# SwiGLU by seven products: eight pairs instead of seven, and ten chunks of the output product instead of nine

## The chip, the cores and the metric

The kernel runs on one core of a Trainium2 chip. The metric is the device time of one execution in microseconds (us), as the median of several runs. TensorE is called PE in the profile, its weight load PEld, VectorE DVE, ScalarE ACT, GpSimd POOL and SyncE SP.

## The reference

One layer of a streaming encoder for 256 rows of 2048 float32 values. What the change touches is the feed-forward part at its end; the mixer ahead of it gives x.

```python
h = rms_norm(x, norm_ffn[l])
gate_up = jnp.einsum('btd,df->btf', h, w_ffn_in[l])      # 2048 -> 2 x 5632
ff_gate, ff_up = jnp.split(gate_up, 2, axis=-1)
x = x + jnp.einsum('btf,fd->btd', jax.nn.silu(ff_gate) * ff_up, w_ffn_out[l])   # 5632 -> 2048
```

Ahead of it stand an RMS norm, one input projection (w_in), a gated recurrence and a chunked attention, their projections (w_pa, w_pb), gates, and an output projection (w_out) with a residual addition.

## The kernel before

**Products in float32.** TensorE multiplies in a reduced format. So every operand is cut in two halves, high and low: ScalarE writes the high half (a cast), VectorE subtracts it from the source for the low half (`load_weights` L151 and L152, `split` L183 and L184). One product of a 128x128 activation tile with a 128x512 weight tile is then a triple of matmuls, high x high, high x low, low x high (L174 to L176 in `product`, L229 to L231 in `product_pair`).

**Tiles.** Weights come by DMA from SP's queue in blocks of 512 KB (`fetch`, tile raw, 8 places): 128 partitions, two k-tiles, 512 columns. The halves have 7 places each (whi, wlo). A chunk is 512 rows of a weight, four k-tiles. The 256 rows of the activations are two row halves m. Activations lie transposed as high and low tiles (xT, x2T, hT), in the pool big, whose 25 places of 4 KB a partition also hold most other tiles.

**Seven products for eight.** `product_pair` does two column blocks at once. In a plain chunk this takes 16 triples. Where a chunk has a form (a tile with sums of its first two k-tiles' activations, made by `act_forms`), `seven` does the first two k-tiles by Strassen's scheme in Winograd's order: seven products of sums for the 2 x 2 x 2 blocks. Four of them (1, 5, 6, 7) are collected over all chunks in four PSUM banks of their own (ub, from the pool u_pool) and added behind the last chunk that has a form (`four_sums`, `residual_sums`); the others go straight to the result banks (cb, from c_pool). PSUM's eight banks are two pools of four, mm and aux. The weights' sums are made by `weight_forms` (L200) on VectorE.

**The stages.** In the feed-forward part, eleven steps j each make one 512-column block of the gate and one of the up part of w_fi over 4 chunks, by `swiglu_pair` where j is in SEVEN_IN and by two plain products otherwise. `here` and `other`, the two PSUM pools, change places at each j. The result hn is transposed by TensorE and split into hT[j] (`transpose_split`, L293, L302, L303). Where two seven pairs follow each other, this step of the first is put off (`late`, list `then`) until the sums of the second. For j in SEVEN the form of hT[j] is made too and written to DRAM (`kept`); for j in AWAY (0 to 3) hT[j] itself is written to DRAM (`put_away`) and loaded back later. Then two pairs of column blocks of w_fo run over the eleven chunks in the order 4 to 10, 0 to 3 (`ORDER`); each loads its forms one by one through `form_loader` (pool form, two places) on SP's queue. `again` loads hT[0..3] and the x for the residual addition on POOL's queue.

**The order of the work.** The instructions of an engine stand in an order that a planner chooses at compile time: by priority, which falls in the order of writing, from a simulation of the times. Weight preparation is written with a raised priority (PREP_AHEAD). Generators that were started move on by one step at each tick; a tick comes after every four triples. A tile that finds no free place in its pool makes its first writer wait. `keep_in_program_order` keeps a DMA on its queue in the written order.

Of the kernel before, what the change touches and what calls it, by code (L numbers as in the profile page):

```python
# [30 lines left out]
NPAR = 58  # L31

PREP_AHEAD = 500
N_WARM = 5

ORDER = (4, 5, 6, 7, 8, 9, 10, 0, 1, 2, 3)
SEVEN = ORDER[1:10]
AWAY = (0, 1, 2, 3)  # L40


SEVEN_IN = (1, 2, 4, 5, 7, 8, 10)
SEVEN_GATE = (1, 3)
SEVEN_OUT = (0,)

# [2 lines left out]
def block_kernel(ctx: ExitStack, tc: tile.TileContext, x, x_t, w_in, w_pa, w_pb, w_out, w_fi, w_fo,  # L49
# [3 lines left out]
    wraw_p = ctx.enter_context(tc.tile_pool(name="wraw", bufs=8))  # L53
    whi_p = ctx.enter_context(tc.tile_pool(name="whi", bufs=7))
    wlo_p = ctx.enter_context(tc.tile_pool(name="wlo", bufs=7))
    big = ctx.enter_context(tc.tile_pool(name="big", bufs=25))
    form_p = ctx.enter_context(tc.tile_pool(name="form", bufs=2))
    small = ctx.enter_context(tc.tile_pool(name="small", bufs=4))
    t6_p = ctx.enter_context(tc.tile_pool(name="t6", bufs=2))
    t2_p = ctx.enter_context(tc.tile_pool(name="t2", bufs=3))  # L60
# [6 lines left out]
    def nm(s):  # L67
        uid[0] += 1
        return f"{s}_{uid[0]}"

    def t4(shape, s, dt=F32):
        return big.tile(shape, dt, tag="t4", name=nm(s))
# [24 lines left out]
    warm_ps = aux.tile([P, 512], F32, tag="bank", name="warm_ps")  # L97
    for _ in range(N_WARM):
        nc.tensor.matmul(warm_ps[:, 0:256], lhsT=warm[:, 0:P], rhs=warm, start=True,
# [22 lines left out]
    def start(g):  # L122
        running.append(g)
# [160 lines left out]
    def split_tiles(s):  # L284
        return (t4([P, 4, T], s + "h", F32R), t4([P, 4, T], s + "l", F32R))
# [29 lines left out]
    def transpose_split(nat, hi, lo, gain=None, wait=2, pool=aux, forms=None, spill=None):  # L315
        for _ in range(wait):
            yield 1
        for pair in range(2):
            pt = transpose_split_pair(nat, pair, hi, lo, gain, pool)
            if forms is not None and pair == 0:  # L320
                act_forms(pt, forms, gain)
                if spill is not None:
                    nc.gpsimd.dma_start(out=spill, in_=forms.bitcast(F32))
            yield 1
# [23 lines left out]
    def form_loader(src):  # L348

        def get():  # L350
            f = form_p.tile([P, 2, 4, P], F32R, tag="form", name=nm("sf"))
            nc.sync.dma_start(out=f.bitcast(F32), in_=src)
            return f
        return get
# [536 lines left out]
    def swiglu_pair(j, c_pool, u_pool, then):  # L891
        hn = t4([P, 2, 512], "hn")
        u = []

        def sums(ub):
            u.extend(t2([P, 512], "u") for _ in range(2))
            four_sums(ub, hn[:, 0, :], hn[:, 1, :], *u)

            for g in then:
                start(g)  # L900

        cb = product_pair(w_fi, (j, NJ + j), 4, act_x2, fx, c_pool, u_pool, sums,
                          plain_first=True, last=True)
        for m in range(2):
            add(hn[:, m, :], cb[m, 0], hn[:, m, :])
            nc.scalar.activation(hn[:, m, :], hn[:, m, :], AF.Silu, scale=r2[:, m:m + 1])
        for m in range(2):
            add(u[m], cb[m, 1], u[m])
            up_times(hn, m, u[m])
        return hn  # L910
# [13 lines left out]
    for j in range(NJ):  # L924
        here, other = pools[j % 2], pools[1 - j % 2]
        if j in SEVEN_IN:
            hn = swiglu_pair(j, here, other, then)
# [10 lines left out]
        f = spill = None  # L938
        if j in SEVEN:
            f = t4([P, 2, 4, P], "sform", F32R)  # L940
            spill = kept[j] = dram.tile([P, 2, 4, P], F32, tag=f"kept{j}", name=nm("kept"))
        seven_next = j + 1 in SEVEN_IN or j + 1 == NJ
        late = j in SEVEN_IN and j + 1 in SEVEN_IN
        g = transpose_split(hn, *hT[j], forms=f, spill=spill, wait=0 if seven_next else 2,
# [9 lines left out]

    def again(nbs, xs, js):

        for _ in range(6):
            yield 1
        for j in js:
            hT[j] = split_tiles("hT")  # L960
            for d, dst in zip(away[j], hT[j]):
                tc.keep_in_program_order(nc.gpsimd.dma_start(out=dst.bitcast(F32), in_=d))
        for nb in nbs:
            xs[nb] = t4([P, 2, 512], "x2")
            tc.keep_in_program_order(nc.gpsimd.dma_start(out=xs[nb], in_=x2_kept[nb]))

    for pair in range(2):
        nbs = (2 * pair, 2 * pair + 1)
        xs = {}
        start(again(nbs, xs, AWAY if pair == 0 else ()))  # L970
        forms = {j: form_loader(kept[j]) for j in SEVEN}
        cb = product_pair(w_fo, nbs, NJ, act_h, forms, pools[1 - pair], pools[pair],
                          residual_sums(xs, nbs), last=pair == 1, chunks=ORDER)
        for n, nb in enumerate(nbs):
            for m in range(2):
                pieces = 2 if nb == 3 and m == 1 else 1
                w = 512 // pieces
                for i in range(pieces):
                    sl = slice(i * w, (i + 1) * w)
                    add(xs[nb][:, m, sl], cb[m, n][:, sl], xs[nb][:, m, sl])  # L980
                    nc.sync.dma_start(out=out_v[:, m, nb * 512 + i * w:nb * 512 + (i + 1) * w],
                                      in_=xs[nb][:, m, sl])
# [63 lines left out]
```

## Time and profile before

| | us |
|---|---|
| median of 3 runs (1418.93 to 1419.85) | 1419.33 |
| the profiled execution | 1418.53 |
| its span, from the first to the last instruction | 1416.5 |
| PE busy in it | 1408.3 |
| VectorE busy | 1119.3 |
| ScalarE busy | 791.7 |

The profile is of one execution. The engines run side by side, so busy times are not added. A row of the timeline gives start, length, engine, line, operation and tiles, with the number of equal instructions merged (x3); in square brackets stands how long the engine was idle before it and what ended that. Matmuls overlap, and the pace is the distance of their starts.

### The profile page before, as it was taken

The numbers are of one execution on the slowest core, as the hardware profiler recorded it, in microseconds if no ns is written. First come the engines' busy times: TensorE is split into PE (matmuls) and PEld (weight loads), VectorE is DVE, ScalarE is ACT, GpSimd is POOL, SyncE is SP. The second block draws the span as 40 slices with busy tenths as digits, with TensorE's granted clock in tenths as the row PEclk, the third lists the DMA queues.
The fourth block names the chain that finished last, engine by engine and source line by source line (L and its number), as shares of the span: only waits on it lengthen the run. The fifth ranks groups of instructions, "written<-read, shape, count | busy, mean of one in ns | idle before, by whom it ended". The sixth has DMA issues, their size and how long they took to land.

```text
span 1416.5 us, 17818 instructions
## 1 busy us (share of the span) xinstructions
PE 1408.3 (99%) x6412; PEld 1170.3 (83%) x6412; DVE 1119.3 (79%) x1459; ACT 791.7 (56%) x1038; POOL 61.1 (4%) x82
## 2 busy tenths in 40 slices
PE   9999999999999999999999999999999999999998
PEld 7888888888888888888888888888888888788887
DVE  6868869555878687779767987998699789889885
ACT  7756655565556464446654655655456455554652
POOL 0100100101100001120000000000000000100000
PEclk9999999999999999999999999999999999999999
DMA  9754454455868566557655677656576646988771
GB/s 359 279 193 160 150 182 156 153 185 189 263 217 296 188 237 237 196 166 236 245 199 178 208 267 253 215 197 221 178 243 236 225 162 209 346 306 313 248 260 56
DMA packets 88327, 311.96 MB, mean 220 GB/s; under 512 B 9904, under 2 KB 10160, under 8 KB 88240
## 3 DMA queue, kind: packets, MB, share of 16 engines
q1 hardware_dynamic: 82016, 288.29, 59.0%
q0 software_dynamic: 6224, 22.55, 4.2%
q8 instruction: 50, 0.82, 0.2%
q14 instruction: 37, 0.30, 0.1%
HBM read 295.60 MB, written 15.20 MB: 219 GB/s over the span
## 4 chain that ended last, share of the span: by engine, by line
PE 98%; DMA 1%; SPq 0%; ACT 0%; issue 0%; DVE 0%; DVEq 0%
PE mm L174 16%; PE mm L176 16%; PE mm L175 16%; PE mp L229 15%; PE mp L230 15%; PE mp L231 15%; PE bank L293 2%; PE bank L559 1%; DMA sf<-kept 1%; DMA xt<-in_x_t 1%; PE bank L589 0%; PE bank L635 0%; PE bank L686 0%; PE bank L714 0%; PE bank L724 0%; PE bank L726 0%
## 5 line engine op out<-in xcount | busy, mean ns | idle before, releaser
L152 DVE TENSOR_TENSOR wlo<-raw,whi 128x1024 fp32r<-128x1024 f32 (+1 forms) x260 | 311.9, 1209 | 132.9 <-ACT whi L151 130.8
L151 ACT CAST whi<-raw 128x1024 fp32r<-128x1024 f32 (+1 forms) x260 | 267.3, 1038 | 232.8 <-PE mm L176 152.4
L183 ACT CAST whi<-raw 128x1024 fp32r<-128x1024 f32 x248 | 230.5, 951 | 175.4 <-PE mp L231 85.9
L184 DVE TENSOR_TENSOR wlo<-raw,whi 128x1024 fp32r<-128x1024 f32 x248 | 267.5, 1098 | 48.5 <-ACT whi L183 47.5
L174 PE MATMUL mm<-whi,xTh 128*128 128x512 f32 x576 | 227.8, 400 | 0.8 <-ACT whi L151 0.8
L176 PE MATMUL mm<-whi,xTl 128*128 128x512 f32 x576 | 225.5, 391 | 0.0
L175 PE MATMUL mm<-wlo,xTh 128*128 128x512 f32 x576 | 225.4, 391 | 0.0
L174 PEld LDWEIGHTS mm<-whi,xTh 128*128 128x128 f32 x576 | 108.6, 189 | 23.0 <-ACT whi L151 2.0
L176 PEld LDWEIGHTS mm<-whi,xTl 128*128 128x128 f32 x576 | 108.5, 188 | 22.7
L175 PEld LDWEIGHTS mm<-wlo,xTh 128*128 128x128 f32 x576 | 108.7, 189 | 21.8 <-DVE wlo L152 0.7
L230 PE MATMUL mp<-wlo,x2Th 128*128 128x512 f32 x308 | 120.4, 391 | 0.0
L231 PE MATMUL mp<-whi,x2Tl 128*128 128x512 f32 x308 | 119.8, 390 | 0.0
L229 PE MATMUL mp<-whi,x2Th 128*128 128x512 f32 x308 | 111.2, 392 | 0.0
L183 ACT CAST whi<-tb 128x1024 fp32r<-128x1024 f32 x58 | 60.9, 1050 | 80.1 <-DVE tb L200 43.5
L230 PE MATMUL mp<-wlo,hTh 128*128 128x512 f32 x262 | 101.9, 389 | 0.0
L231 PE MATMUL mp<-whi,hTl 128*128 128x512 f32 x262 | 101.9, 389 | 0.0
L174 PE MATMUL mm<-whi,x2Th 128*128 128x512 f32 x256 | 100.0, 391 | 0.0
L175 PE MATMUL mm<-wlo,x2Th 128*128 128x512 f32 x256 | 99.8, 390 | 0.0
L176 PE MATMUL mm<-whi,x2Tl 128*128 128x512 f32 x256 | 99.8, 390 | 0.0
L184 DVE TENSOR_TENSOR wlo<-ta,whi 128x1024 fp32r<-128x1024 f32 x58 | 70.8, 1220 | 35.8 <-ACT whi L183 35.7
L229 PE MATMUL mp<-whi,hTh 128*128 128x512 f32 x262 | 97.0, 389 | 0.0
L183 ACT CAST whi<-ta 128x1024 fp32r<-128x1024 f32 x58 | 60.9, 1050 | 51.0 <-PE mp L231 28.6
(257 smaller groups left out, 2406.4 us busy)
## 6 DMA issues: line engine op xcount, KB each, us to landing
raw<-in_w_fi SPq DMA_DIRECT2D x176, 512.0 KB, 4.9
raw<-in_w_in SPq DMA_DIRECT2D x172, 512.0 KB, 4.3
raw<-in_w_fo SPq DMA_DIRECT2D x88, 512.0 KB, 5.4
raw<-in_w_out SPq DMA_DIRECT2D x32, 512.0 KB, 4.8
sf<-kept SPq DMA_DIRECT2D x18, 512.0 KB, 6.0
raw<-in_w_pa SPq DMA_DIRECT2D x16, 512.0 KB, 4.5
raw<-in_w_pb SPq DMA_DIRECT2D x16, 512.0 KB, 4.5
kept<-sform POOLq DMA_DIRECT2D x9, 512.0 KB, 4.4
```

The source lines that it names most:

```text
L151: nc.scalar.copy(hi[:, sl, :], src[:, sl, :])
L152: nc.vector.tensor_tensor(out=lo[:, sl, :], in0=src[:, sl, :], in1=hi[:, sl, :].bitcast(F32), op=ALU.subtract)
L174: nc.tensor.matmul(ps[m], lhsT=ah, rhs=wh, start=kc == 0 and k4 == 0, stop=False)
L175: nc.tensor.matmul(ps[m], lhsT=ah, rhs=wl, start=False, stop=False)
L176: nc.tensor.matmul(ps[m], lhsT=al, rhs=wh, start=False, stop=kc == n_chunks - 1 and k4 == 3)
L183: nc.scalar.copy(hi, src)
L184: nc.vector.tensor_tensor(out=lo, in0=src, in1=hi.bitcast(F32), op=ALU.subtract)
L229: nc.tensor.matmul(ps, lhsT=ah, rhs=wh, start=first, stop=False)
L230: nc.tensor.matmul(ps, lhsT=ah, rhs=wl, start=False, stop=False)
L231: nc.tensor.matmul(ps, lhsT=al, rhs=wh, start=False, stop=final)
L293: nc.tensor.transpose(out=pt[:, j, m * P:(m + 1) * P], in_=nat[:, m, c:c + P], identity=ident)
L559: nc.tensor.matmul(pl[:, j, :], lhsT=ek[:, g // 2, (g % 2) * P:(g % 2 + 1) * P], rhs=eq[:, g, :], start=True, stop=True)
```

## The change

The list of seven pairs becomes 1, 2, 3, 5, 6, 7, 9, 10: eight instead of seven, with three in a row twice. The output product's chunk 3, the last of the order, also gets a form, so that ten of eleven chunks are done by seven products, and the sums of the collected banks move into that last chunk. The pool form gets a third place and big loses one. `again` waits five ticks ahead of each of the four hT blocks and of x, where it waited six ticks once and then loaded all. One more warm-up product (128x256, on zeros) stands at the start.

```diff
-N_WARM = 5
+N_WARM = 6
 ORDER = (4, 5, 6, 7, 8, 9, 10, 0, 1, 2, 3)
-SEVEN = ORDER[1:10]
+SEVEN = ORDER[1:]
 AWAY = (0, 1, 2, 3)
-SEVEN_IN = (1, 2, 4, 5, 7, 8, 10)
+SEVEN_IN = (1, 2, 3, 5, 6, 7, 9, 10)
@@
-    big = ctx.enter_context(tc.tile_pool(name="big", bufs=25))
-    form_p = ctx.enter_context(tc.tile_pool(name="form", bufs=2))
+    big = ctx.enter_context(tc.tile_pool(name="big", bufs=24))
+    form_p = ctx.enter_context(tc.tile_pool(name="form", bufs=3))
@@ def again(nbs, xs, js):
-        for _ in range(6):
-            yield 1
         for j in js:
+            for _ in range(5):
+                yield 1
             hT[j] = split_tiles("hT")
             for d, dst in zip(away[j], hT[j]):
                 tc.keep_in_program_order(nc.gpsimd.dma_start(out=dst.bitcast(F32), in_=d))
+        for _ in range(5):
+            yield 1
         for nb in nbs:
             xs[nb] = t4([P, 2, 512], "x2")
```

## Rows read from the trace of the kernel before

**Rows 1.** The page: busy us, share of the span, instructions of each engine.

```profile
PE 1408.3 (99%) x6412; PEld 1170.3 (83%) x6412; DVE 1119.3 (79%) x1459; ACT 791.7 (56%) x1038; POOL 61.1 (4%) x82
```

**Rows 2.** Waits of PE, whole run: us in total, times, longest.

```profile
PE mp L229 <- DMA sf<-kept: 2.4, 1, 2.4
PE warm_ps L99 <- DVE warm L96: 1.2, 1, 1.2
PE mm L174 <- ACT whi L151: 0.8, 2, 0.7
```

**Rows 3.** Timeline of PE in the last chunk: start us, length us, instruction.

```profile
1404.35 0.39 PE L229 MATMUL mp<-whi,hTh 128*128 128x512 f32 x1
...
1405.03 0.39 PE L229 MATMUL mp<-whi,hTh 128*128 128x512 f32 x1
```

**Rows 4.** Windows: length, then busy us by engine, PEclk, DMA share, GB/s.

```profile
798.00:839.50 41.50, 41.50 (x187) 34.30 (x187) 39.78 (x47) 25.13 (x28) 0.00 (x0) 1.00 0.61 205
839.50:862.00 22.50, 22.50 (x107) 18.76 (x105) 17.26 (x28) 12.47 (x17) 2.66 (x5) 1.00 0.78 273
...
1305.00:1395.00 90.00, 90.00 (x399) 74.55 (x398) 76.20 (x84) 51.89 (x54) 0.00 (x0) 1.00 0.65 222
```

**Rows 5.** The chain of waits, 1205 to 1230 us: start, length, what.

```profile
1214.65 8.41 DMA sf<-kept
```

**Rows 6.** Waits of SP's queue, 1183 to 1300 us: us in total, times, longest.

```profile
SPq L352 <- PE mp L231: 31.4, 8, 7.6
```

**Rows 7.** Timeline of POOL: first and last load of the burst, 11 in all.

```profile
1212.45 0.53 POOL L962 DMA_DIRECT2D hTh<-h  x1
...
1225.63 0.53 POOL L965 DMA_DIRECT2D x<-x  x1 [1.93 <-issue]
```

**Rows 8.** Windows, the stretch behind that burst (columns as in rows 4).

```profile
1222.00:1246.00 24.00, 22.89 (x101) 18.97 (x102) 17.82 (x20) 11.92 (x13) 1.06 (x2) 1.00 1.03 418
```

**Rows 9.** Tile hTh on PE: length ns min/median/max, first and last start us.

```profile
L229 PE MATMUL mp<-whi,hTh x262: 389/389/476, 1181.8 to 1411.8; 128*128 128x512 f32 x131
```

**Rows 10.** Timeline of DVE in steady w_fo.

```profile
1336.70 0.68 DVE L200 TENSOR_TENSOR ta<-raw 128x512 f32<-128x512 f32 x1
1337.30 1.22 DVE L184 TENSOR_TENSOR wlo<-raw,whi 128x1024 fp32r<-128x1024 f32 x1
1338.44 0.68 DVE L200 TENSOR_TENSOR tb<-ta,raw 128x512 f32<-128x512 f32 x1
```

**Rows 11.** Timelines of DVE and PE, early in pair j=2.

```profile
810.47 3.49 DVE L184 TENSOR_TENSOR wlo<-raw,whi 128x1024 fp32r<-128x1024 f32 x3
...
814.60 0.39 PE L230 MATMUL mp<-wlo,x2Th 128*128 128x512 f32 x1
```

**Rows 12.** Timeline of PE at the start.

```profile
1.18 4.63 PE L99 MATMUL warm_ps<-warm 128*128 128x256 f32 x10 [1.18 <-DVE warm L96]
...
6.49 1.22 PE L174 MATMUL mm<-whi,xTh 128*128 128x512 f32 x2 [0.67 <-ACT whi L151]
...
14.04 0.73 PE L174 MATMUL mm<-whi,xTh 128*128 128x512 f32 x2 [0.16 <-ACT whi L151]
```

**Rows 13.** Timeline of DVE at the end: the last addition.

```profile
1412.71 0.76 DVE L103 TENSOR_TENSOR x<-mp,x 128x256 f32<-128x256 f32 x2 [2.03 <-PE mp L231]
```

**Rows 14.** Timelines of DVE and PE, from pair j=2 to pair j=3.

```profile
837.17 0.68 DVE L103 TENSOR_TENSOR hn<-mp,u 128x512 f32<-128x512 f32 x1
...
839.70 0.48 PE L174 MATMUL mm<-whi,x2Th 128*128 128x512 f32 x1
...
840.49 0.40 PE L174 MATMUL mm<-whi,x2Th 128*128 128x512 f32 x1
840.70 0.68 DVE L103 TENSOR_TENSOR u<-mp,u 128x512 f32<-128x512 f32 x1
...
842.43 0.68 DVE L303 TENSOR_TENSOR hTl<-bank,hTh 128x512 fp32r<-128x512 f32 x1
...
846.74 0.28 DVE L333 TENSOR_TENSOR sf<-bank,sf 128x128 f32<-128x128 f32 x1
```

## The prediction

> **What bounds the kernel now.** I read the page's busy shares first: TensorE is busy 1408.3 us of a 1416.5 us span, VectorE 79%, ScalarE 56% [rows 1]. A busy TensorE need not be at its peak, so I looked at its waits next: 4.4 us in the whole run, of which 2.4 us is one wait for a loaded activation form and 1.2 us is the start [rows 2]. Between them TensorE issues product after product at an even pace: the first matmul of one triple is at 1404.35 us, that of the next at 1405.03, so a triple of three 128x512 matmuls takes 0.68 us and one matmul 0.2267 us (the 0.39 us in a row is its length in the pipeline, not its pace) [rows 3]. So the end is set by the count of matmuls, plus 2.4 us. What could take over is VectorE, which makes the weight halves: where two seven-product pairs follow each other it is busy 39.78 of 41.5 us, against 17.26 of 22.5 in the plain pair after them [rows 4]. The argument below is therefore: count the matmuls removed, take off the one wait if its cause goes, and ask whether VectorE, PSUM or the DMA give it back.
>
> **Removed products.** A plain 512-row chunk over two column blocks needs 2 blocks x 4 k-tiles x 2 row halves = 16 triples; the seven-product form replaces 8 by 7, so 15. SEVEN_IN grows from 7 to 8 pairs: 4 chunks. SEVEN grows from 9 to 10 chunks, used by both output pairs: 2 chunks. 6 triples x 0.68 = 4.08 us, all on TensorE and therefore on the path.
>
> **The wait for a loaded form (2.37 us).** The chain of waits shows the form of one chunk issued on SP at 1214.65 us and landing 8.41 us later, when TensorE has already stopped [rows 5]. Two things made it late. Its issue waited for a place: with two places, form loads wait for TensorE to finish an older form, 31.4 us in 8 waits [rows 6]. And from 1212.45 to 1225.63 us POOL issues 8 h tiles and 3 x tiles of 512 KB, one burst [rows 7]; in the 24 us after it the DMA engines are full at 418 GB/s [rows 8]. With a third place the load of one chunk can be issued a chunk (15 triples, 10.2 us) earlier, which is more than the 2.37 us it was late. With five ticks (20 triples, 13.6 us) between the h pieces, 4 to 8 of the 11 transfers of the burst, at 512 KB / 418 GB/s = 1.25 us each, move out from in front of it: 5 to 10 us. Either alone covers 2.37. Bounds: 0 (the wait reappears on a weight block) to -2.37; I take -2.37, because two independent reliefs are each larger.
>
> **h in pieces, moved on POOL.** The first product pair of w_fo starts at 1181.8 us [rows 9]. The pieces are allowed at ticks 5, 10, 15, 20 (about 1196, 1209, 1223, 1237 us), x at tick 25 (1250 us). Block 0 is used from triple 106 (1254 us), block 3 from triple 151 (1285 us), x in the sums behind it. Behind a waiting h load on POOL's queue stand only the later h and x loads. Each has some 35 us or more from its tick to its use; were that cover gone, TensorE would wait for the landing itself.
>
> **More work on VectorE.** A full weight half is 1.22 us long and followed 1.14 us later, a form operation 0.68 and 0.60 [rows 10]. A plain chunk is 4 halves, 4.6 us; a seven chunk 5 halves, one short one and 4 form operations, 5 x 1.14 + 5 x 0.60 = 8.7 us. Six chunks: 24.6 us more in VectorE's time. In a seven chunk TensorE takes 10.2 us, so it is hidden by itself; steady w_fo shows this, 76.2 us busy in 90 with TensorE never idle [rows 4]. The extra form of block 3 (4 x 0.28 + 0.68, about 1.8 us) falls in the plain pair j=4, where VectorE has 5 us free in 22.5 [rows 4].
>
> **Three in a row.** New is a third seven pair (j=3, j=7) straight after a second whose delayed transposes have just run. That leaves VectorE two lower halves of h and one form, 2 x 0.68 + 4 x 0.28 + 0.68 = 3.2 us (lengths of [rows 10, 14]), in the third pair's beginning, where before a plain pair had room: 39.8 + 3.2 = 43.0 us against TensorE's 41.5. The stock of prepared halves is the reserve. Pairing the tiles that VectorE finishes with the triples in written order, the thinnest place in a second pair is a half finished at about 811.7 us (the first of three) and used at 814.60 [rows 11]: 2.9 us. So the worst case is 2.9 - 3.2, a stall of 0.3 us and, with what reordering could add, about 1.2 us at each of two places; the best is nothing, since weights are prepared at a raised priority and the 3.2 us can be done later. Bounds 0 to 2.4, I take 0.6.
>
> **Start.** Ten warm-up matmuls end at 5.81 us; one more product is two matmuls of 0.46, to 6.74, and the first real product, which starts at 6.49, comes 0.25 us later. At 14.04 TensorE waits for the second block's weights and activations anyhow [rows 12]; the wait of 0.16 there hides most of it. It can gain nothing either, because that block's x decides. Bounds 0 to 0.25, I take 0, since 0.09 at most is left.
>
> **End.** The last chunk is now a seven chunk, so its sums start 9 triples (6.1 us) before TensorE's end. They are 7 additions after the last of the four sum products, then 4 final ones ahead of the last: 11 at the 0.60 of rows that follow each other [rows 10] is 6.6 us, against 6.1 minus 0.2 for the last result to arrive. The last addition, which before waits for TensorE alone [rows 13], may come up to 0.7 us later, and the output pieces are nearer together. Bounds 0 to 1; I take 0.3.
>
> **One place less in big** (24) and two more form loads, one more spill: no wait of TensorE comes from a place there. Counting live tiles in the code, the tightest stage of the feed-forward part (8 x2T, 4 fx, 10 hT, hn, sform) needs 24. I take 0; a late place would appear as part of the 0.6 or 2.4 above.
>
> **Sum.** The profiled execution took 1418.53 us (span 1416.5 and 2.0 around it); the median of the runs is 1419.33, 0.80 above. 1418.53 - 4.08 - 2.37 + 0.6 + 0.3 = 1412.98, and 0.80 on top: **1413.8 us**. The same without any give-back and with the other 0.8 us of waits on ScalarE gone is 1419.33 - 4.08 - 2.37 - 0.8 = 1412.1, the lowest.
>
> **Rivals.** (B) *The wait moves.* Without the stop of 2.4 us TensorE arrives that much sooner at weight blocks that come through the same crowded DMA, and stops there. Then only the products count: 1419.33 - 4.08 + 0.3 = 1415.6, up to 1416.4. For it: weights and forms share the full DMA. Against: the burst itself is thinned.
>
> (C) *The memory rate is the limit.* From 1212 to 1256 us the changed kernel must move 44 / 10.2 = 4.3 chunks of 4 weight blocks and a form, and 10 h and x tiles: 31.6 transfers, 39.5 us at the 1.25 us of the trace, which fits. Were the rate one seventh lower, it would not fit by about 2.3 us, the reserve of halves would be gone with it, and the stop would stay: 1419.33 - 4.08 + 0 to 2.3, about 1416.6. The rows speak against it: 418 GB/s for 24 us [rows 8]. The Trainium skill (DMA: Bandwidth & Descriptors, Where 436 GB/s comes from) has such a rule: loads from HBM are bound at about 358 GB/s per core, and by it this case would hold. The trace does not agree, 418 was held.
>
> (D) *The third pair starves.* The 0.6 above becomes 1.2 to 2.5 us at each of the two places, as VectorE's debt of 1.5 us per third pair adds to the 3.2 us: 2.4 to 5 in all, so 1413.8 - 0.6 + 2.4 to 5 = 1415.6 to 1418.2.
>
> (E) *Slower: PSUM banks at the third pair.* The delayed transposes use two of the four banks in which j=3 now needs all four at once (a plain product needed two). On the clock of before the banks come free at 837.9, 841.4, 843.1 and 847.0 us (ends of the last readers [rows 14]), and j=3 starts at 839.7. If TensorE's order were the written one (each k-tile for both row halves, then the other column block), it would stop 1.0 us for the second bank and 2.9 us for the fourth, and up to 4.1 more because VectorE now prepares a seven chunk first: 3.9 to 8 us at j=3 and j=7 each, up to 5 when w_fo starts behind j=10. 8 to 21 us, about 12: 1413.8 + 12 = 1425.8. It decides from 8.5 us on. Against it: the planner reorders. At 840.49 TensorE begins j=3's second triple while, by the same count, only one bank is free [rows 14], so that triple went into the first bank and not into the written one; in a seven chunk 13 of 15 triples need no fourth bank.
>
> That the third place is not used, as form loads stand behind weight loads on SP, gives B's time.
>
> **Chances.** Forecast 0.60 (its own range 1412.1 to 1415.0), B 0.17, C 0.06, D 0.11, E 0.06. A measurement of this kernel tells about 0.2% from no change, 2.84 us, so faster means below 1416.5. Faster: 0.60 + 0.17 + 0.02 of C + 0.04 of D = 0.83. Same: 0.04 + 0.07 = 0.11. Slower: E, 0.06. The range 1412.1 to 1417.4 leaves out E and part of D and C, about 0.12.
>
> **What the changed profile would show.** Matmuls 18 fewer, two warm-up matmuls more; the waits of TensorE without the form; POOL's h loads in steps of about 13 us and the DMA share below 1.0 between 1215 and 1245 us; VectorE busy above 40 us in the windows of j=3 and j=7 without a wait of TensorE. If TensorE waits for weights at the start of j=3 and j=7, it is D; for VectorE's reads of banks there, E; for weight blocks in the first third of w_fo, B or C. The prediction is wrong if waits of more than 1.2 us in all appear in one of these places, or if the pace of 0.2267 us per matmul changes.

## The result and the profile after

The changed kernel takes 1412.21 us (median of 5 runs, 1411.78 to 1412.92); the kernel before, in the 5 runs that stand beside it, 1418.93 us (1417.15 to 1419.85). The recorded ratio is 0.9949 (95% interval 0.9936 to 0.9963; the two medians alone give 0.9953): 0.5% faster. The forecast was 1413.8 us, against 1419.33 a ratio of 0.9961, and 0.9949 was the lowest ratio of its range; the measurement lies at that lower end, so the direction was right and the gain was forecast too small. Later runs on one chip gave 1412.58 us against 1420.54, ratio 0.9945 (0.9932 to 0.9957).

The profiled execution took 1412.02 us, its span 1410.2. The page's busy times, which answer to [rows 1]:

```profile
PE 1403.2 (100%) x6396; PEld 1165.1 (83%) x6396; DVE 1148.9 (81%) x1508; ACT 800.1 (57%) x1053; POOL 61.7 (4%) x83
```

TensorE has 16 instructions fewer: 18 matmuls less and 2 of the warm-up more. VectorE has 29.6 us more, against 24.6 + 1.8 in the forecast.

The waits of TensorE over the whole run, which answer to [rows 2]; columns are total us, times, longest:

```profile
PE mm L174 <- ACT whi L151: 1.4, 2, 1.2
PE warm_ps L99 <- DVE warm L96: 1.2, 1, 1.2
PE mp L229 <- DVE u L103: 0.4, 1, 0.4
```

The wait for a loaded form is gone. The wait on whi lies ahead of the first real product. One new wait of 0.4 us has come: TensorE waits for a VectorE addition that reads a PSUM bank. It stands at the start of w_fo, in PE's timeline:

```profile
1182.18 0.50 PE L229 MATMUL mp<-whi,hTh 128*128 128x512 f32 x1 [0.45 <-DVE u L103]
```

The start, which answers to [rows 12]:

```profile
1.18 4.33 PE L99 MATMUL warm_ps<-warm 128*128 128x256 f32 x12 [1.18 <-DVE warm L96]
...
6.68 0.73 PE L174 MATMUL mm<-whi,xTh 128*128 128x512 f32 x2 [1.17 <-ACT whi L151]
...
12.95 0.73 PE L174 MATMUL mm<-whi,xTh 128*128 128x512 f32 x2 [0.19 <-ACT whi L151]
```

The second chunk starts at 12.95 us instead of 14.04. Two things came earlier together. TensorE still waits there for weights and activations of that chunk, as before, so their arrival moved. And TensorE's own pace differs: in the kernel before its first products follow each other 0.43 us apart, about half the pace of the rest, until some 10 us; here it is 0.23. The timeline of PE before, then of the changed kernel:

```profile
8.36 0.63 PE L175 MATMUL mm<-wlo,xTh 128*128 128x512 f32 x1
8.79 0.63 PE L176 MATMUL mm<-whi,xTl 128*128 128x512 f32 x1
```

```profile
7.97 0.40 PE L175 MATMUL mm<-wlo,xTh 128*128 128x512 f32 x1
8.21 0.39 PE L176 MATMUL mm<-whi,xTl 128*128 128x512 f32 x1
```

The profile's granted clock reads 1.00 in both stretches, so that here the pace alone tells them apart; in experiment 3 it reads 0.50 at the same pace of 0.43.

Windows of the changed kernel: pair j=2, the third pairs j=3 and j=7 (their borders from the plain pairs' matmuls), and the first part of w_fo with the burst of loads. Columns are the window, its length, busy us of PE, PEld, DVE, ACT, POOL, the granted clock, DMA share, GB/s; they answer to [rows 4, 8]:

```profile
797.10:838.50 41.40, 41.40 (x187) 34.23 (x187) 41.40 (x52) 24.89 (x29) 0.00 (x0) 1.00 0.63 210
838.50:880.00 41.50, 41.50 (x187) 34.21 (x186) 41.31 (x53) 25.92 (x31) 1.60 (x3) 1.00 0.67 234
...
1008.30:1049.70 41.40, 41.40 (x187) 34.24 (x186) 41.10 (x53) 26.62 (x32) 0.53 (x1) 1.00 0.62 223
...
1204.00:1246.00 42.00, 42.00 (x187) 34.79 (x186) 34.20 (x39) 23.30 (x25) 5.84 (x11) 1.00 1.00 385
```

In the third pair VectorE has next to no idle time (41.31 of 41.50 us, 41.10 of 41.40), and TensorE none. How near it was is seen in the timelines of DVE and PE, the thinnest place of j=3 (the pairing in written order of [rows 11]): a half finished at 851.22 + 1.22 = 852.44 us is used at 853.48, 1.05 us later.

```profile
851.22 1.22 DVE L184 TENSOR_TENSOR wlo<-tb,whi 128x1024 fp32r<-128x1024 f32 x1
...
853.48 0.39 PE L230 MATMUL mp<-wlo,fx 128*128 128x512 f32 x1
```

The end, which answers to [rows 13], in the timelines of DVE and PE:

```profile
1403.32 3.73 DVE L103 TENSOR_TENSOR x<-mp,x 128x512 f32<-128x512 f32 x7
...
1405.81 0.39 PE L231 MATMUL mp<-whi,hTl 128*128 128x512 f32 x1
```

VectorE's last addition ends at 1407.05 us, 1.24 us behind the start of the last matmul. Before it was 1413.47 [rows 13] - 1412.29 = 1.18, by PE's timeline:

```profile
1412.29 0.39 PE L231 MATMUL mp<-whi,hTl 128*128 128x512 f32 x1
```

The span ends 4.39 us behind that start instead of 4.21.

Where the 6.3 us of span went: 18 matmuls x 0.2267 = 4.08 less, the wait for the form 2.37 less, the start 1.09 less, the bank wait 0.45 more, the end 0.18 more. This makes 6.91; the missing 0.6 lies in gaps of 0.2 us and less that I could not put down to one cause. Whether the start is the change's doing is not settled (experiments 1 and 4). Without it, from the start of the second chunk to the end, the two profiles are 1402.46 and 1397.25 us long, 5.2 apart; that length is 1397.34 in the profiles of experiments 1 and 11 too, so it is the start that differs between profiles of nearly the same kernel.

### The profile page after: what moved, and what is told of

Read it like the earlier page. It is cut to its first block, busy times and chain, and to the rows that moved or that the text cites. A ratio compares the mean times of both kernels' runs of the same rounds, so it can differ in the third digit from the quotient of the medians.

```text
span 1410.2 us, 17862 instructions
## 1 busy us (share of the span) xinstructions
PE 1403.2 (100%) x6396; PEld 1165.1 (83%) x6396; DVE 1148.9 (81%) x1508; ACT 800.1 (57%) x1053; POOL 61.7 (4%) x83
## 4 chain that ended last, share of the span: by engine, by line
PE 97%; DVE 1%; issue 1%; DMA 0%; ACT 0%; SPq 0%; DVEq 0%
PE mp L229 16%; PE mp L231 15%; PE mp L230 15%; PE mm L174 15%; PE mm L176 15%; PE mm L175 15%; PE bank L293 2%; PE bank L559 1%; DMA xt<-in_x_t 0%; PE bank L589 0%; DVE x L103 0%; PE bank L635 0%; PE bank L686 0%; DVE u L103 0%; DVE wlo L184 0%
## 5 line engine op out<-in xcount | busy, mean ns | idle before, releaser
L152 DVE TENSOR_TENSOR wlo<-raw,whi 128x1024 fp32r<-128x1024 f32 (+1 forms) x244 | 293.3, 1211 | 121.3 <-ACT whi L151 120.7
L151 ACT CAST whi<-raw 128x1024 fp32r<-128x1024 f32 (+1 forms) x244 | 250.7, 1037 | 215.7 <-PE mm L176 151.9
L183 ACT CAST whi<-raw 128x1024 fp32r<-128x1024 f32 (+1 forms) x264 | 243.1, 947 | 163.9 <-PE mp L231 81.5
L184 DVE TENSOR_TENSOR wlo<-raw,whi 128x1024 fp32r<-128x1024 f32 (+1 forms) x264 | 283.2, 1094 | 40.0 <-ACT whi L183 39.2
L230 PE MATMUL mp<-wlo,x2Th 128*128 128x512 f32 x352 | 137.8, 391 | 0.0
L231 PE MATMUL mp<-whi,x2Tl 128*128 128x512 f32 x352 | 137.0, 390 | 0.0
L183 ACT CAST whi<-tb 128x1024 fp32r<-128x1024 f32 x64 | 67.2, 1050 | 109.1 <-DVE tb L200 72.9
L229 PE MATMUL mp<-whi,x2Th 128*128 128x512 f32 x352 | 125.4, 391 | 0.0
L184 DVE TENSOR_TENSOR wlo<-ta,whi 128x1024 fp32r<-128x1024 f32 x64 | 78.1, 1220 | 29.6 <-ACT whi L183 29.4
L184 DVE TENSOR_TENSOR wlo<-tb,whi 128x1024 fp32r<-128x1024 f32 x64 | 78.2, 1221 | 6.2 <-ACT whi L183 4.9
L229 PEld LDWEIGHTS mp<-whi,x2Th 128*128 128x128 f32 x352 | 66.1, 188 | 14.2 <-DVE u L103 0.2
L231 PEld LDWEIGHTS mp<-whi,x2Tl 128*128 128x128 f32 x352 | 66.1, 188 | 13.5
```

What stands on the lines that cost most here:

```text
L151: nc.scalar.copy(hi[:, sl, :], src[:, sl, :])
L152: nc.vector.tensor_tensor(out=lo[:, sl, :], in0=src[:, sl, :], in1=hi[:, sl, :].bitcast(F32), op=ALU.subtract)
L183: nc.scalar.copy(hi, src)
L184: nc.vector.tensor_tensor(out=lo, in0=src, in1=hi.bitcast(F32), op=ALU.subtract)
L229: nc.tensor.matmul(ps, lhsT=ah, rhs=wh, start=first, stop=False)
L230: nc.tensor.matmul(ps, lhsT=ah, rhs=wl, start=False, stop=False)
```

## The experiments

The theories: mine was that the gain is the count of matmuls plus the wait for a form, which goes by two reliefs (the third place, the h loads in pieces), and that three pairs in a row are borne by the stock of prepared halves. Against it stood that the warm-up product gained the 1.09 us at the start, that one of the reliefs does nothing, and that three in a row is no special case since the planner always finds other work. "The changed kernel" below has 1412.2 to 1412.6 us. The kernel before had a median of 1420.06 us (17 runs) on the chip of experiments 1 to 4, by chance the same 1420.06 (21 runs) on that of 5 to 8, and 1420.54 (9 runs) on that of 9 to 11. The changed kernel itself was run on other chips than those of 1 to 8, so its distance from those is best read from the ratios.

**1. One warm-up product fewer.**

```diff
-N_WARM = 6
+N_WARM = 5
```

> The changed kernel with five warm-up products instead of six, nothing else. Landing theory: the second chunk starts when its x block has landed and been cut, whatever TensorE did before, so the time stays within 0.3 us of the changed kernel (1412.2 us, ratio to the kernel before about 0.9955 on one chip). Warm-up theory: the sixth product is what made the start 1.09 us earlier (14.04 to 12.95 us), so this kernel is 0.5 to 1.1 us slower than the changed one and its second chunk starts near 14.0 us.

Measured: 1413.0 us (1411.96 to 1413.88, 6 runs), ratio 0.9951 (0.9939 to 0.9963). In its profile the second chunk starts at 14.06 us, as the warm-up theory said, but it waits 0.81 us for its weights there: TensorE had been ready.

```profile
14.06 0.73 PE L174 MATMUL mm<-whi,xTh 128*128 128x512 f32 x2 [0.81 <-ACT whi L151]
```

So in this execution it was not TensorE that was late; its first products run at the full pace here, with five warm-up products. The time speaks for neither theory beyond its spread.

**2. Two places for forms again.**

```diff
-    big = ctx.enter_context(tc.tile_pool(name="big", bufs=24))
-    form_p = ctx.enter_context(tc.tile_pool(name="form", bufs=3))
+    big = ctx.enter_context(tc.tile_pool(name="big", bufs=25))
+    form_p = ctx.enter_context(tc.tile_pool(name="form", bufs=2))
```

> The changed kernel with two places for loaded forms and 25 in big, as before; all else changed. If the third place took the wait for a form away, the wait of some 2.4 us comes back: 1414.6 us, and the wait row of TensorE for sf returns. If the other order of the loads of h did it, or the burst merely fell differently, no wait for sf above 0.5 us and a time within 0.5 us of the changed kernel.

Measured: 1413.53 us (1412.2 to 1414.01, 6 runs), ratio 0.9954 (0.994 to 0.9967). The wait is back, at half its length, in the waits of TensorE:

```profile
PE mp L229 <- DMA sf<-kept: 1.1, 1, 1.1
```

The third place takes this wait away. In the changed kernel it is worth 1.1 us in the profile and about as much in the median, not 2.4. That it is less here I put down to when the burst falls on a form, as in experiment 6; no run separates this. The edit also gives big its place back; no wait of TensorE in these profiles names a place in big, but its size was not changed alone.

**3. The h loads written as before.**

```diff
-        for j in js:
-            for _ in range(5):
-                yield 1
+        for _ in range(6):
+            yield 1
+        for j in js:
             hT[j] = split_tiles("hT")
...
-        for _ in range(5):
-            yield 1
         for nb in nbs:
```

> The changed kernel with the h loads written as before: six ticks once, then all. If ticks keep the loads apart on the chip, this brings the burst back and costs up to 2.4 us. The trace of the changed kernel shows its h loads in one burst all the same (six from 1208.06 to 1211.08 us), so my theory is now that a tick sets a place in the written order and no wait: no change, within 0.5 us of 1412.2, and the h loads at the same times.

Measured: 1413.35 us (1412.64 to 1413.73, 5 runs), ratio 0.9953 (0.994 to 0.9967), no wait for a form. POOL's timeline of this kernel, then that of the changed one, first, sixth and seventh of the h loads:

```profile
1209.78 0.53 POOL L962 DMA_DIRECT2D hTh<-h  x1
...
1212.79 0.54 POOL L962 DMA_DIRECT2D hTl<-h  x1
1218.27 0.53 POOL L962 DMA_DIRECT2D hTh<-h  x1 [4.94 <-DMA kept<-sform]
```

```profile
1208.06 0.53 POOL L962 DMA_DIRECT2D hTh<-h  x1
...
1211.08 0.54 POOL L962 DMA_DIRECT2D hTl<-h  x1
1217.53 0.53 POOL L962 DMA_DIRECT2D hTh<-h  x1 [5.91 <-DMA kept<-sform]
```

The two are alike: 3.0 us from the first to the sixth in both, then a pause that ends with the write of a form (kept<-sform). Ticks put the loads at another place in the written order, and nothing makes the queue wait for TensorE to get there. The piecewise loading had no part in the gain that these runs can tell. The median is 0.8 to 1.1 us above the changed kernel's, where at most 0.5 was expected. The profile has this at the start: the second chunk begins at 15.02 us, and the granted clock of the first products, the column ahead of the DMA share, is 0.50:

```profile
9.00:11.50 2.50, 2.50 (x7) 1.93 (x6) 0.78 (x3) 1.24 (x2) 0.00 (x0) 0.50 0.94 335
```

From there to the end it takes 1396.9 us, no more than the changed kernel.

**4. The kernel before with six warm-up products.**

```diff
-N_WARM = 5
+N_WARM = 6
```

> The kernel before with six warm-up products, nothing else. Landing theory: within 0.3 us of the kernel before on the same chip. Warm-up theory: 0.5 to 1.1 us faster than the kernel before, with the second chunk starting near 13.0 instead of 14.0 us.

Measured: 1418.97 us (1417.54 to 1420.83, 12 runs) against 1420.06 (1416.92 to 1422.94, 17 runs), ratio 0.9993 (0.9984 to 1.0001): no effect that is clear of the spread. The second chunk starts at 13.32 us here, at the full pace. Over all 13 profiles this start lies between 12.95 and 15.02 us. Only in three (before, changed, experiment 1) does the profile show TensorE waiting there, 0.16 to 0.81 us; in the others TensorE itself comes last. What sets it then is when the first product starts (6.5 to 7.9 us) and whether the first products run some 3 us at half the pace: they do in five of the six profiles with five warm-up products (not in experiment 1) and in two of the seven with six (experiments 3 and 8). This leans to the warm-up theory, as do both medians (0.4 to 1.1 us), but one execution of each kernel does not settle it.

This profile showed what I had not looked for. The windows around the wait for a form, 2.4 us long here too:

```profile
1219.00:1223.40 4.40, 1.98 (x9) 1.32 (x8) 1.23 (x1) 0.47 (x2) 1.06 (x2) 1.00 1.03 419
1223.40:1226.80 3.40, 3.40 (x9) 2.68 (x8) 1.23 (x1) 1.99 (x3) 0.53 (x1) 0.50 1.02 386
1226.80:1230.20 3.40, 3.40 (x16) 2.81 (x15) 2.96 (x5) 2.88 (x4) 0.53 (x1) 1.00 1.03 420
```

Behind the stop the granted clock is 0.50, the 1.2 GHz level, for 3.4 us, and TensorE does 9 matmuls in place of 16. In the profiled execution of the kernel before the same stop was followed by the full clock:

```profile
1223.10:1226.50 3.40, 3.39 (x15) 2.82 (x16) 1.23 (x1) 2.06 (x3) 1.06 (x2) 1.00 1.03 420
```

So the stop costs its length in one execution, and by this estimate 1.7 us more (half of 3.4) in another. This became the new theory for the missing gain.

**5. The kernel before with the third place, products unchanged.**

```diff
-    big = ctx.enter_context(tc.tile_pool(name="big", bufs=25))
-    form_p = ctx.enter_context(tc.tile_pool(name="form", bufs=2))
+    big = ctx.enter_context(tc.tile_pool(name="big", bufs=24))
+    form_p = ctx.enter_context(tc.tile_pool(name="form", bufs=3))
```

> The kernel before with a third place for loaded forms and 24 in big, nothing else (products unchanged). If the third place is enough to take the wait for a form away, TensorE has no wait for sf and the time falls by 2.4 us, or by up to 4 us in executions in which the clock had dropped behind that wait: a ratio of 0.997 to 0.998. If the wait moves to a weight block instead, a wait of 1 to 2.4 us on whi or wlo near 1225 to 1265 us and a ratio of 0.999 to 1.000.

Measured: 1415.6 us (1415.27 to 1416.65, 5 runs) against 1420.06 (1417.03 to 1421.98, 21 runs), ratio 0.9968 (0.9956 to 0.9981): 4.5 us, with not one matmul fewer. Its waits of TensorE are those of the start alone:

```profile
PE warm_ps L99 <- DVE warm L96: 1.2, 1, 1.2
PE mm L174 <- ACT whi L151: 1.0, 1, 1.0
```

The wait went and did not move to a weight block, though the burst stands at the same place (h loads from 1212.05 us). The timelines of SP's queue show why: the kernel before loads two forms ahead of w_fo (992.70 and 1037.76 us) and the third at 1214.65, in the burst; here the third goes out at 1113.74, some hundred us before its use. The spread went too, from 5 us in 21 runs to 1.4 in 5. This term, which I had at 2.37, is worth about as much as the products (4.08). In the two profiles, which both have the full clock in w_fo, the part from the second chunk on is 3.05 us shorter: 2.37 is the wait, the other 0.7 I could not place.

**6. The kernel before with the eight pairs alone.**

```diff
-SEVEN_IN = (1, 2, 4, 5, 7, 8, 10)
+SEVEN_IN = (1, 2, 3, 5, 6, 7, 9, 10)
```

> The kernel before with the eight seven pairs 1,2,3,5,6,7,9,10, nothing else: two places for forms, h at once, nine chunks of the output product. 12 matmuls of 0.2267 us fewer, 2.72 us. If three in a row costs nothing, 2.7 us faster, ratio 0.998, without a wait of TensorE at the third pairs; the wait for a form in w_fo should stay, at 1 to 2.4 us. If the third pairs starve, 0 to 1.5 us faster only, with waits at the starts of j=3 and j=7.

Measured: 1415.55 us (1413.63 to 1417.04, 5 runs), ratio 0.9965 (0.9951 to 0.9978), 4.5 us instead of 2.7. No wait at j=3 or j=7; the waits of TensorE behind the start:

```profile
PE mp L229 <- DMA sf<-kept: 0.8, 1, 0.8
PE mp L229 <- DVE u L103: 0.4, 1, 0.4
```

The form was late by 0.8 us only; I read this as w_fo having moved with the shorter pairs. The gain is then the 2.7 us of the products and 1.6 of the stop's length, less 0.4 for a bank, 3.9 of the 4.5; behind the short stop the clock stays at 1.00. The 0.4 us bank wait stands at the start of w_fo (1183.72 us), behind the pairs 9, 10; without the eight pairs (experiments 5 and 7) it is not there.

**7. The kernel before with ten chunks alone.**

```diff
-SEVEN = ORDER[1:10]
+SEVEN = ORDER[1:]
```

> The kernel before with ten instead of nine chunks of the output product by seven products, nothing else. 6 matmuls fewer, 1.36 us. At the end VectorE's sums lie behind the last products: 0 to 0.7 us back. So 0.7 to 1.4 us faster, ratio 0.999 to 0.9995, with the last addition at most 0.7 us behind the last matmul's end.

Measured: 1418.12 us (1415.1 to 1420.9, 11 runs), ratio 0.9986 (0.9976 to 0.9996), 1.9 us with an interval from 0.6 to 3.4; 0.7 to 1.4 was expected. The stop for the form (2.3 us) is there in its profile and takes the clock with it, in the second of these windows:

```profile
1219.00:1222.90 3.90, 1.78 (x8) 1.13 (x6) 2.00 (x3) 1.05 (x1) 0.53 (x1) 1.00 0.98 382
1222.90:1226.30 3.40, 3.24 (x8) 2.56 (x9) 0.48 (x1) 1.04 (x1) 0.53 (x1) 0.51 1.02 411
```

The last addition ends at 1413.79 us, 1.25 behind the start of the last matmul at 1412.54: the sums behind the last products cost 0.07 us at most there.

**8. Nine pairs, in runs of four and five.**

```diff
-SEVEN_IN = (1, 2, 3, 5, 6, 7, 9, 10)
+SEVEN_IN = (1, 2, 3, 4, 6, 7, 8, 9, 10)
```

> The changed kernel with nine seven pairs, 1,2,3,4 and 6,7,8,9,10: four and five in a row. Another 12 matmuls fewer, 2.72 us. By the theory that VectorE's stock of prepared halves is the limit: it was down to 1.05 us (j=3) and 1.55 us (j=7) in the changed kernel with VectorE busy 41.0 of 41.0 us, so a fourth and a fifth pair run it out, TensorE waits for wlo or whi some 1 to 3 us in each of the pairs j=4, 9 and 10, 3 to 6 us in all, and the kernel is not faster than the changed one (0 to +3 us). By the rival that the planner always finds other work to do in time: no such waits, 1409.5 us.

Measured: 1417.59 us (1415.56 to 1419.48, 11 runs), ratio 0.9986 (0.9976 to 0.9996): 12 matmuls fewer than the changed kernel and about 5 us slower than it, where 0 to 3 was expected. (The 41.0 of 41.0 us there is of a window that begins 9 us ahead of j=3.) The waits of TensorE behind the start, and two that stand behind the transposes between j=8 and 9 and between j=9 and 10:

```profile
PE mp L229 <- DVE hn L103: 2.8, 3, 1.4
...
PE mp L230 <- DVE wlo L184: 1.8, 3, 0.6
```

```profile
1096.52 0.50 PE L229 MATMUL mp<-whi,x2Th 128*128 128x512 f32 x1 [1.15 <-DVE hn L103]
...
1141.16 0.50 PE L229 MATMUL mp<-whi,x2Th 128*128 128x512 f32 x1 [1.41 <-DVE hn L103]
```

The fourth and fifth pairs stop TensorE in both ways at once: for PSUM banks that VectorE has not yet read (2.8 us in three waits) and for lower halves (1.8 us in three). This is 4.6 us; with 2.7 off for the products, and 0.4 for the bank wait that the changed kernel has and this one has not, 1.5 us more than the changed kernel would be left. Its span is 5.4 longer. The start holds 1.8 of the rest: the second chunk begins at 14.77 us instead of 12.95, with the granted clock at 0.50 in the first products. Behind the stops between the pairs it stays at 1.00. Some 2 us stay open.

**9. Nine pairs, three in a row three times.**

```diff
-SEVEN_IN = (1, 2, 3, 5, 6, 7, 9, 10)
+SEVEN_IN = (0, 1, 2, 4, 5, 6, 8, 9, 10)
```

> The changed kernel with nine seven pairs in three runs of three: 0,1,2 and 4,5,6 and 8,9,10. As many products as the kernel with nine pairs in runs of four and five, 12 matmuls (2.72 us) fewer than the changed one. If a third pair in a row is what the stock of prepared halves can bear and a fourth is not, there are no waits of TensorE at j=2, 6 and 10 above 0.5 us each and the time is 2 to 2.7 us below the changed kernel, some 1410 us. If the limit is VectorE's total work instead, or the start of w_fo straight behind a third pair, 1 to 4 us of waits eat it up.

Measured: 1412.04 us (1411.9 to 1412.62, 5 runs), ratio 0.9941 (0.9928 to 0.9955); the changed kernel beside it 1412.58. The third pairs have no wait on wlo:

```profile
PE mp L229 <- ACT x2Th L308: 1.1, 1, 1.1
PE mp L229 <- DVE sf L333: 0.4, 1, 0.4
```

But its first pair, j=0, comes straight behind w_out, and TensorE waits 1.1 us there for the activations of the last block (at 748.79 us), and 0.4 for a bank. These 1.5 us, less the 0.4 of the changed kernel, are half of what is missing: of the 2.7 only half a microsecond was left, and 1.1 I could not place. That is within the spread of both, so it is not shown to beat the changed kernel, and the expected 2 to 2.7 us did not come. The limit is where the pairs stand in a row, and not VectorE's total work, since this kernel has as many seven pairs as that of experiment 8.

**10. One place for forms.**

```diff
-    big = ctx.enter_context(tc.tile_pool(name="big", bufs=25))
-    form_p = ctx.enter_context(tc.tile_pool(name="form", bufs=2))
+    big = ctx.enter_context(tc.tile_pool(name="big", bufs=26))
+    form_p = ctx.enter_context(tc.tile_pool(name="form", bufs=1))
```

> The kernel before with one place for loaded forms instead of two and 26 in big: the cost of a late form by itself. Each of the 9 forms of each output pair can then be issued only when TensorE is done with the one before it, 4 to 8 us ahead of its use or less, while a load takes 3.2 to 6 us outside the burst and 8 to 12 in it: stops of TensorE near the burst of more than 2.4 us, some smaller ones elsewhere, 5 to 20 us in all. By the theory that a stop can also take the clock down for a while behind it, the rows behind stops of 2 us and more show matmuls at a pace of 0.43 us in some stretches and the time is longer than the sum of the waits; by the rival that the stop is all it costs, the pace behind every stop is 0.2267.

Measured: 1435.38 us (1434.74 to 1436.91, 4 runs) against 1420.54, ratio 1.0107 (1.0092 to 1.0121), 14.8 us slower. Its waits of TensorE, without the start:

```profile
PE mp L229 <- ACT whi L183: 3.7, 3, 1.5
PE mp L229 <- DMA sf<-kept: 3.3, 1, 3.3
PE mp L230 <- DVE wlo L184: 2.5, 3, 1.0
...
PE mp L229 <- DMA sf<-fq: 0.9, 1, 0.9
```

and its windows in the first part of w_fo:

```profile
1204.00:1214.90 10.90, 9.44 (x41) 7.28 (x39) 9.27 (x14) 6.30 (x7) 2.23 (x5) 1.00 0.62 200
1215.40:1225.60 10.20, 6.47 (x14) 4.63 (x15) 4.14 (x6) 2.05 (x2) 3.73 (x7) 0.50 1.02 411
1225.60:1235.80 10.20, 8.31 (x36) 6.31 (x35) 6.37 (x7) 3.82 (x5) 0.53 (x1) 1.00 1.02 410
1235.90:1239.20 3.30, 3.30 (x10) 2.53 (x9) 2.76 (x4) 1.05 (x1) 0.00 (x0) 0.50 1.00 403
1239.30:1249.40 10.10, 8.21 (x36) 6.22 (x35) 5.59 (x6) 4.73 (x5) 0.00 (x0) 1.00 0.81 277
1249.50:1260.00 10.50, 10.50 (x40) 8.46 (x40) 6.75 (x9) 4.73 (x5) 0.00 (x0) 0.84 0.46 165
```

The waits are 10.4 us, 8.0 more than the 2.4 of the kernel before; 6.2 of them are for weight halves and not for a form. The median is 14.8 more, and the profiled span 16.5. Of the 8.5 us between the spans that are no waits, 6.6 are the clock by this estimate: half of TensorE's busy time at 0.50, (6.47 + 3.30) / 2 = 4.9, and 0.16 x 10.5 = 1.7 in the last window. The other 1.9 I could not place. The clock fell three times: in the second of two stops of 1.46 and 0.95 us (to 1214.42 and 1215.87 us), and twice behind two stops of 1.14 and 0.76 us (the last to 1234.99 and to 1249.28), with half a microsecond of work between the two each time. The stop of 3.3 us lies inside the first stretch at 0.50. So the rival that a stop costs its length alone falls.

**11. The changed kernel once more,** beside 9 and 10, with no edit.

> The changed kernel itself, on the same chip as the others of this call and with more runs. If the two heaps in the times of the kernel before (near 1418 and near 1421 us) come from the clock behind its stop of 2.4 us, the times of this kernel, which has no such stop, lie within 1.5 us of each other, near 1412 to 1413.5 us, and the ratio to the kernel before is 0.9945 to 0.9960.

Measured: 1412.58 us (1412.11 to 1413.21, 5 runs), ratio 0.9945 (0.9932 to 0.9957). Its five times lie within 1.1 us; the nine of the kernel before beside them spread from 1418.06 to 1422.02. This is as the theory has it, but no execution of the upper heap was traced.

## Why the prediction was right or wrong

**What bounds the kernel: right.** Away from the start and from stretches at a lower clock TensorE kept its pace of 0.2267 us per matmul. What I could place of the changes of the time was a change of its count, of its waits, or of its clock; 0.6 to 2 us in several profiles stay open.

**Removed products: right in size.** 4.08 us in the forecast; the profile has the 18 matmuls fewer. Experiments 6 and 7 each gained more than their 2.72 and 1.36 us, but in experiment 6 the stop changed too, and the interval of 7 reaches from 0.6 to 3.4, so they confirm the sign and not the second digit.

**The wait for a form: the step that failed.** I took it at its length in one profiled execution, 2.37 us, and made this the outer bound too ("0 to -2.37"). Taken away alone (experiment 5) it is worth 4.5 us of the median, with an interval from 2.7 to 6.2. What I left out is what stands behind a stop: the granted clock may fall to 0.50, as experiments 4, 7 and 10 show, and 3.4 us at half the clock is 1.7 us. The profile that I worked from had no such stretch in w_fo ([rows 4], [rows 8]), and so one execution could not tell me. In the executions of the kernel before that have a mean granted clock of 1.000, on the chip of experiments 5 to 8, the median is 1418.2 us (8 of 21), 6 us above the changed kernel; my terms without the clock, 4.08 + 2.37 - 0.45 - 0.18, make 5.8. The other 13 have a median of about 1421. That it is this stop which parts them is argued and not shown: no execution of the upper heap was traced, the mean clock falls as well by a drop at the start (experiments 3, 6, 7, 8) or behind the last matmul, where it costs nothing (experiment 11), and some near 1421.5 with a mean clock of 0.999 are slower than one stretch of 1.7 us explains.

**The two reliefs: one of two.** The third place was right (experiments 2 and 5). The h loads "in steps of about 13 us" were wrong: they went out in one burst at 1208 us, and experiment 3 without the new ticks is alike. I had read ticks as times, and a tick is a place in the written order. The third form went out a hundred us earlier and not the one chunk of 10.2 us that I had reckoned (experiment 5). The DMA share stayed at 1.00 between 1204 and 1246 us, where I had said it would be below; the stop went all the same, because the form in need had been loaded before the burst.

**More work on VectorE, three in a row: right, and nearer than the forecast cost.** 43.0 us of need in a third pair against 41.5 of time was seen as 41.31 of 41.50 busy. The reserve was to fall from 2.9 to about -0.3 us; by the same pairing in written order it fell to 1.05. I gave 0.6 us for it and it cost nothing. Experiment 8 shows the edge one pair further, experiment 9 that the third is borne wherever it stands.

**Rival E, the banks: the mechanism is there, at 0.45 us** in place of 8 to 21, and only where w_fo starts behind j=10 (up to 5 us there in the forecast), not at j=3. The planner put other products first, as the argument against it said. In experiment 8 it is the larger of the two stops.

**End: right.** 0.18 us measured for 0.3 taken.

**Start: a second term that was mis-sized.** I took it at 0, with a cost of up to 0.25 us as its only bound, because the landing of x decides. It was 1.09 us shorter in the profiles compared, more than the whole distance between the measured and the forecast span there: from the second chunk on the gain is 5.2 us, a little less than my 5.55. The landing decides in three of 13 profiles; in the others TensorE is the later one, and the half pace of its first products, which stands in [rows 12] (two matmuls of 128x512 in 1.22 us, later in 0.73), costs it some 1.3 us. I had read the waits of these rows and not their lengths. The first product did not wait for the sixth warm-up product either: it waited 1.17 us for its weights. Whether that product keeps the first ones at the full pace is not settled (experiments 1 and 4), and so part of the gain may be luck.

**Rivals B, C and D** did not come. For B and C the rows are those of the changed kernel and of experiment 5: a DMA share of 1.00 and 0.94 over 42 us from 1204 us, and no wait for a weight. 418 to 420 GB/s was held again in several kernels (experiment 4), so C's lower rate is not this core's.

**The sum** was short by the stop and the start: give-backs of 0.9 were 0.6, the stop was worth about 2 us more than its length in the median of experiment 5, and the start 1.09 us in the profiles. How the result's own runs share between these two is open, since only one execution of the kernel before was traced.

## What to carry to other kernels

Price a stop of a bound TensorE by its length and by the granted clock of the few microseconds behind it, and look at more than one execution: the times of the kernel before fell into two heaps, and its profile showed one of them. Read the lengths of the first matmuls as well as their waits. A third buffer that lets a load go out ahead of a burst was worth 4.5 us (2.7 to 6.2) by itself, as much as all the arithmetic of the change (4.08); in the changed kernel, where the form was later by 1.1 us only, it was worth about that. Such terms do not simply add. Where a helper engine works ahead, follow the stock (finish to use) through the worst stretch: it bore three pairs and not four, and no busy share of the whole run would have said so.

## What the runs showed of the hardware that was not expected

A stop of TensorE of 2.4 and 2.3 us was followed by 3.4 us at a granted clock of 0.50 in two kernels (experiments 4 and 7), and not in the profiled execution of the kernel before with the same stop. Stops of 1.15 and 1.41 us in experiment 8 and of 1.1 us in experiment 2 were not followed by a drop; two of 1.14 and 0.76 us close to each other in experiment 10 were. In experiment 10 a stretch at 0.50 lasted from 1215.4 to 1225.6 us, with TensorE busy 6.47 of 10.2 us in it. At the start of a run the first products went at half the pace for some 3 us in seven of 13 profiles, in four of them with a granted clock of 0.50 on record (experiments 3, 6, 7 and 8).
